# Seven products in place of eight: Strassen's algorithm in one feed-forward stage of a two-layer diffusion backbone

## The chip, the core and the metric

The kernel runs on one core of a Trainium2 chip. The metric is the device time of one execution in microseconds (us). The engines are TensorE (PE in the profile, with PEld for its weight loads), VectorE (DVE), ScalarE (ACT), GpSimd (POOL) and SyncE (SP), which issues the DMAs. Every engine works through its own instructions in their order and waits on semaphores for the others.

## The reference

Two layers work on 512 latent tokens and 256 context tokens, 768 in all, of 1024 channels. Each layer is a feed-forward block (FFN), a mixer and a second FFN. Cut to what matters here:

```python
def half_ffn(x, shift, scale, gate, w1, w3, w2):
    h = modulate(x, shift, scale)
    return x + 0.5 * gate * ((jax.nn.silu(h @ w1) * (h @ w3)) @ w2)
```

`w1` and `w3` (the up projections) are 1024 x 2816, `w2` (the down projection) is 2816 x 1024, all in float32. The first FFN of each layer treats latent and context tokens with the same weights and with different shift, scale and gate.

## The kernel before

Everything is kept with channels on the 128 partitions and tokens along the free dimension. A matrix product in float32 is made of three matmuls on float32r parts: each operand is split into a high part (a rounded copy) and a low part (the operand less that copy), and `mmk` issues high x high, high x low and low x high for each of the k tiles (128 channels each).

**Weights.** The weight tiles (128 x 1024, 512 KB) are used in a planned list, `w_items`. `w_dma` (L190) lets SyncE load one into one of four `raw` buffers. `w_split` (L196) has ScalarE write the high part (L202) and VectorE subtract for the low part (L209, or L207 where it is emitted late). `w_next` (L211) hands out the next tile and first emits the loads and splits that lie ahead of it: with four `hi` and `lo` buffers, up to two tiles ahead.

**The FFN.** The 2816 inner channels are 22 blocks of 128, taken in chunks of 4, 4, 4, 4, 2, 4 blocks. `f1` (L488) does one block: it takes its w1 tile, multiplies it with the context tokens (256 columns) and the latent ones (512 columns), 8 k tiles x 3 matmuls each, lets ScalarE apply silu (L476), does the same with w3, and `gate` (L479) multiplies the two on VectorE (L484), has ScalarE copy the high part (L485) and VectorE subtract for the low part (L486). A block is thus 96 matmuls. `f2` (L513) does the down projection of a whole chunk: for m = 0 to 7 and each group of tokens `down` (L503) sums the chunk's blocks in PSUM, and VectorE adds the result with its gate to the residual (`scalar_tensor_tensor`, L511). `f2` of one chunk is emitted after the first block of the next. The last chunk's is merged with the beginning of the next stage (`post`). PSUM has four buffers for the up projections (`psa`) and four for the down projections (`psb`).

The order of the work is the order in which the program emits it: nothing is reordered. Layer 1's first FFN is the call with `post=self.rw_begin`. Its first two blocks, `first_block`, run while the tokens are being normalised. During layer 0's FFNs and the first part of layer 1 other work, the layers' modulation, is taken from a list `bg` by `ticks`; in layer 1's first FFN that list is empty. The tiles that live through a stage, the activations' parts among them, are 45 slabs of 128 x 768.

Of the kernel before, what the change touches and what calls it, by code (L numbers as in the profile page):

```python
# [7 lines left out]
F32 = mybir.dt.float32  # L8
# [131 lines left out]

class K:
# [10 lines left out]
    # ---------- pools  # L152
# [33 lines left out]
    # ---------- weights  # L186
# [24 lines left out]
    def w_next(self, key, live=0):  # L211
        i = self.w_i
        assert self.w_items[i][0] == key, (self.w_items[i][0], key)
        last = min(i + self.W_SP - 1 - live - 1, len(self.w_items) - 1)
        while self.w_s <= max(last, i):
            while self.w_d <= min(self.w_s + self.W_RAW - 1, len(self.w_items) - 1):
# [4 lines left out]
        while self.w_d <= min(self.w_s + self.W_RAW - 1, len(self.w_items) - 1):  # L221
            self.w_dma(self.w_d)
            self.w_d += 1
        self.w_i += 1
        return self.w_sp.pop(i)
# [28 lines left out]
    # ---------- adaLN  # L254
# [17 lines left out]
    def ada_first(self):  # L272
        """shift and scale of the first FFN, half of the channels at a time: every product on the tensor engine, four column groups at once"""
# [53 lines left out]
    # ---------- norm + modulation: h = x * rsqrt(mean(x^2) + eps) * scale + shift  # L327
# [89 lines left out]
    # ---------- SwiGLU  # L417
    def ffn_items(self, l, i):
        A = self.A
        it = []  # L420
        off = f = 0
# [47 lines left out]
    def ffn(self, l, i, groups, h, post=None, first=None):  # L469
        nc = self.nc  # L470
        gd = 2 if i == 0 else 8
        gs = {}

# [14 lines left out]
        def f1(f, nt):  # L488
# [6 lines left out]
            w = self.w_next(("w3", l, i, f))  # L495
            pss = [self.psa() for g in groups]
# [16 lines left out]
        def f2(c, f0, cf):  # L513
            w = None
            for m in range(8):
                if m % (8 // cf) == 0:
                    w = self.w_next(("w2", l, i, c, m * cf // 8))
# [5 lines left out]
        pend = None  # L523
        for c, cf in enumerate(CHUNKS):
            q = 0
            if c == 0 and first is not None:
# [54 lines left out]
                q = 2  # L581
            while q < cf:
# [10 lines left out]
        c, f0, cf = pend  # L593
        if post is None:
# [31 lines left out]
    # ---------- MLA || conv mixer  # L626
# [40 lines left out]
    def mla(self, h, norm_lat):  # L667
# [54 lines left out]
        # the first two blocks of the convolution's input run while the latent tokens are normalised  # L722
# [34 lines left out]
        # latent projections: kv, q, rope key  # L757
# [58 lines left out]
        # token-major q, k, v  # L816
# [11 lines left out]
        def rot(dst, src, w, t, n, eng):  # L828
            """gain and rotation of n tables' tokens; src and dst [128, n, 32], t the first table, or None where nothing turns"""
# [27 lines left out]
        def prep(p):  # L857
            """closures: transposes, split and row maxima of one pair of heads"""
# [129 lines left out]
        self.plan(self.wout_items() + self.ffn_items(0, 1) + self.ffn_items(1, 0) + self.rwkv_items())  # L988
# [72 lines left out]
        def fin(p):  # L1061
            """closures: one over the sums, and the outputs split"""
# [181 lines left out]
        # output projection  # L1244
# [16 lines left out]
        # the attention's half of the rows first; the first NH blocks of the latent tokens go with the context's  # L1261
# [45 lines left out]
    # ---------- RWKV-7 mixer (second layer)  # L1307
# [22 lines left out]
    def rw_sum(self, kt, g):  # L1330
        """the sum of a token's neighbours"""
# [10 lines left out]
    def rw_diff(self, kt, g):  # L1342
        """half the sum, less the token"""
# [19 lines left out]
    def rw_begin(self, st):  # L1363
        """the context's share of the first products, on the side of the last FFN products"""
# [17 lines left out]
    def rwkv_gemm(self, st):  # L1382
# [101 lines left out]
        def pair(n, j, nxt, at):  # L1484
            """two weight tiles, k outermost; the mixes make room for the next ones"""
# [22 lines left out]
        # keys, and their heads' lengths  # L1508
# [39 lines left out]
        # receptances, and the low-rank branches between them  # L1548
# [77 lines left out]
    def rwkv_prep(self):  # L1626
# [34 lines left out]
        # every operation of this phase as a task of one engine; the order of the tasks is that of a greedy schedule  # L1661
# [5 lines left out]
        def task(key, engs, dur, fn, deps=(), take=(), give=(), u=0, lat=0.2):  # L1667
            """engs: where it may run, dur: how long on each; take, give: the buffers that it claims and frees"""
# [8 lines left out]
        def last(z, key, n):  # L1677
            """a tile that n tasks read"""
# [32 lines left out]
        def dir_tasks(u):  # L1711
# [53 lines left out]
            def k_b():  # L1765
                """b = -2 kk a, from t = tanh(./2), a = (1 + t) / 2"""
# [40 lines left out]
            def gram(b):  # L1807
                """the two heads' products of steps 4b .. 4b + 3 and 12 + 4b .. 12 + 4b + 3"""
# [202 lines left out]
    def run_tasks(self, tasks, free, eng, step, bias, off):  # L2011
        """greedy list schedule: an engine takes the most urgent task whose inputs and buffers are there; then all are emitted in the order of their starts"""
# [47 lines left out]
    def t_batch(self, h, b, eng=None, steps=False):  # L2060
        """(I - L)^-1 of eight steps, both directions and half of the heads: one 32 x 32 block per lane"""
# [31 lines left out]
        def q_mul(x, os=(0, 1)):  # L2093
            """8 x 8 blocks below the diagonal's: W = T L, X = W T"""
# [71 lines left out]
    def t_ticks(self, cost):  # L2166
        """the next of the inverses' operations, as many as hold VectorE for so long"""
# [11 lines left out]
    def rwkv_scan(self):  # L2179
# [11 lines left out]
        def load(g, n):  # L2191
            """two steps of one direction and half of the heads"""
# [545 lines left out]
```

## Time and profile before

| | us |
|---|---|
| median of 3 runs | 3438.64 |
| lowest and highest | 3436.89, 3441.31 |
| profiled execution, first to last instruction (its span; what lies around it isn't given) | 3438.3 |
| TensorE busy | 3168.0 (92%) |
| VectorE busy | 2069.5 (60%) |
| ScalarE busy | 1141.4 (33%) |
| GpSimd busy | 663.6 (19%) |

The profile is that of one execution. In it times run from the first instruction. A row of the timeline gives the start, the duration, the engine, the line of the kernel and the operation with its output and inputs; in brackets stands the idle time before it and what ended it. A matmul's duration reaches from its start to the modelled arrival of its result, so the durations of consecutive matmuls overlap.

### The profile page before, as it was taken

To read this page: it belongs to the slowest core of one execution; us is meant where nothing else is said; L and a number is where in the kernel's file an instruction comes from. 1 tells how busy PE (TensorE), PEld (TensorE's weight loads), DVE (VectorE), ACT (ScalarE), POOL (GpSimd) and SP (SyncE) were. 2 spreads that over 40 slices of the span, in tenths; PEclk is the share of its full clock that TensorE was granted. 3 is DMA by queue.
4 is the path that set the end of the run, shared out by engine and by line. 5 is a ranking of instruction groups with operands and counts; after the bars stand their busy time and mean duration, and the time that the engine had idled before them with its cause. 6 is when DMAs were issued, how large, how long until landed. Compare 5 with 4: busy or idle time off the path is not lost. (4 is left out here: it accounts for less than half of the span.)

```text
span 3438.3 us, 51746 instructions
## 1 busy us (share of the span) xinstructions
PE 3168.0 (92%) x21064; PEld 2636.7 (77%) x21064; DVE 2069.5 (60%) x3246; ACT 1141.4 (33%) x2060; POOL 663.6 (19%) x464
## 2 busy tenths in 40 slices
PE   7999999988989999999999999998786477789999
PEld 6888888874578888888888888776554367678887
DVE  5877734798667776555333343637899775663443
ACT  4122213455543211124122113335564245532222
POOL 1000001356320000002000001215787142230000
PEclk9999999999999999999999999999777689989999
DMA  6444311200133444431111111322587788733222
GB/s 242 146 150 147 132 68 62 78 25 1 47 108 129 141 140 150 146 111 56 68 62 62 62 68 62 109 89 95 149 213 201 186 186 184 165 127 103 98 98 80
DMA packets 251374, 390.59 MB, mean 114 GB/s; under 512 B 67328, under 2 KB 136576, under 8 KB 251136
## 3 DMA queue, kind: packets, MB, share of 16 engines
q1 hardware_dynamic: 251136, 387.28, 36.7%
q8 instruction: 166, 2.72, 0.3%
q14 instruction: 72, 0.59, 0.1%
HBM read 323.24 MB, written 63.96 MB: 113 GB/s over the span
## 5 line engine op out<-in xcount | busy, mean ns | idle before, releaser
L233 PE MATMUL psa<-hhi,whi 128*128 128x512 f32 (+1 forms) x2584 | 893.5, 346 | 6.0 <-ACT whi L202 3.9
L233 PE MATMUL psa<-hlo,whi 128*128 128x512 f32 (+1 forms) x2584 | 894.8, 346 | 2.5 <-POOL hlo L385 2.2
L233 PE MATMUL psa<-hhi,wlo 128*128 128x512 f32 (+1 forms) x2584 | 892.1, 345 | 0.0
L209 DVE TENSOR_TENSOR wlo<-wraw,whi 128x1024 fp32r<-128x1024 f32 (+3 forms) x300 | 366.9, 1225 | 450.5 <-ACT whi L202 450.5
L233 PEld LDWEIGHTS psa<-hhi,whi 128*128 128x128 f32 x2584 | 490.0, 190 | 69.7 <-ACT whi L202 3.9
L233 PEld LDWEIGHTS psa<-hlo,whi 128*128 128x128 f32 x2584 | 489.2, 189 | 67.1 <-POOL hlo L385 4.1
L233 PEld LDWEIGHTS psa<-hhi,wlo 128*128 128x128 f32 x2584 | 489.6, 189 | 61.3
L202 ACT CAST whi<-wraw 128x1024 fp32r<-128x1024 f32 (+2 forms) x345 | 344.6, 1009 | 337.1 <-PE psb L233 198.2
L233 PE MATMUL psb<-ghi,whi 128*128 128x512 f32 (+1 forms) x1232 | 425.6, 345 | 1.4 <-DVE xb L511 0.9
L233 PE MATMUL psb<-glo,whi 128*128 128x512 f32 (+1 forms) x1232 | 424.8, 345 | 0.0
L233 PE MATMUL psb<-ghi,wlo 128*128 128x512 f32 (+1 forms) x1232 | 424.5, 345 | 0.0
L342 POOL TENSOR_TENSOR nacc<-nacc,nsq 128x512 f32<-128x512 f32 (+1 forms) x50 | 56.2, 1125 | 1579.0 <-ACT nsq L338 1574.0
L476 ACT ACTIVATE fs<-psa 128x512 f32<-128x512 f32 (+1 forms) x152 | 77.3, 509 | 576.3 <-PE psa L233 576.2
L485 ACT CAST ghi<-fs 128x512 fp32r<-128x512 f32 (+1 forms) x154 | 81.7, 530 | 552.7 <-DVE fs L484 552.7
L233 PEld LDWEIGHTS psb<-ghi,whi 128*128 128x128 f32 x1232 | 231.9, 188 | 32.8 <-issue 2.2
L233 PEld LDWEIGHTS psb<-ghi,wlo 128*128 128x128 f32 x1232 | 232.0, 188 | 30.0
L233 PEld LDWEIGHTS psb<-glo,whi 128*128 128x128 f32 x1232 | 231.8, 188 | 30.0 <-DVE glo L486 0.3
L484 DVE TENSOR_TENSOR fs<-fs,psa 128x512 f32<-128x512 f32 (+1 forms) x149 | 85.1, 571 | 200.5 <-PE psa L233 197.5
L511 DVE SCALAR_TENSOR_TENSOR xb<-psb,mod,xb 128x256 f32<-128x256 f32 (+1 forms) x192 | 115.7, 614 | 124.5 <-PE psb L233 124.4
L268 DVE CUSTOM_DVE_ANT_0 adaj<-adat,sc,vec 128x512 bf16<-128x512 f32 x224 | 167.9, 750 | 14.7 <-DMA adat<-ada 9.1
L268 DVE CUSTOM_DVE_ANT_0 adaj<-adat,sc,mod 128x512 bf16<-128x512 f32 x224 | 167.9, 750 | 5.9 <-DMA adat<-ada 0.3
L233 PE MATMUL psb<-rhs,lhs 96*32 96x64 f32 (+1 forms) x2560 | 81.1, 241 | 70.4 <-DVE prod L2104 21.4
(398 smaller groups left out, 4907.7 us busy)
## 6 DMA issues: line engine op xcount, KB each, us to landing
wraw<-w SPq DMA_DIRECT2D x264, 512.0 KB
adat<-ada SPq DMA_DIRECT2D x256, 256.0 KB
la_d<-AR SPq DMA_DIRECT2D x32, 384.0 KB
kb_d<-KT SPq DMA_DIRECT2D x16, 768.0 KB
lg_d<-G SPq DMA_DIRECT2D x32, 384.0 KB
lhs<-la_d SPq DMA_DIRECT2D x48, 256.0 KB
lhs<-lg_d SPq DMA_DIRECT2D x48, 256.0 KB
kb<-kb_d SPq DMA_DIRECT2D x48, 256.0 KB
```

Source lines behind the costliest of these rows:

```text
L202: nc.scalar.copy(hi, raw)
L209: nc.vector.tensor_tensor(lo, raw, hi, ALU.subtract)
L233: self.last = self.nc.tensor.matmul(ps, lhsT=lhsT, rhs=rhs, start=start, stop=stop)
L268: nc.vector.tensor_tensor_reduce(out=junk, in0=t, in1=self.sc[cd][hf], scale=1.0, scalar=o if hf else self.col("ada_b", l * 72 + j), op0=A ...
L342: (eng or nc.gpsimd).tensor_tensor(st["acc"], st["acc"], sq, ALU.add)
L476: nc.scalar.activation(s, ps[:, 0:grp[1]], AF.Silu)
L484: nc.vector.tensor_tensor(s, s, ps[:, 0:n], ALU.mult)
L485: nc.scalar.copy(ghi[:, t0:t0 + n], s)
L511: nc.vector.scalar_tensor_tensor(xs, ps[:, 0:n], self.modc(l, gd, m, cd), xs, ALU.mult, ALU.add)
```

## The change

For the last 18 of the 22 blocks, two neighbouring blocks' tiles of one matrix (w1, then w3) are taken as a 2 x 2 matrix: rows are the two blocks, columns the two halves of the 1024 channels. The tokens, all 768 of both kinds, are cut into two halves of 384. The eight half-size products become seven, in the form with four sums on each side (Winograd's variant): A11, A12, S4, S1, S2, S3 and A22 name the weight operand of each. One product is 4 k tiles x 3 matmuls of 384 columns.

- The token side's sums are formed once, by `sums()`: 12 closures in `bg`, taken by the ticks of blocks 2 and 3, and four more (`one`) under the first `f2`. Three of them take 12 more slabs; the fourth is written over a part of `h`.
- The weight side's sums are formed for every pair by VectorE, partly in place in the raw tile. Each operand is 128 x 512 and is split as before; two operands share one `hi` and `lo` tile (a unit). A w2 tile is a unit by itself, loaded through one buffer (`raw2`). `ahead()`, called by every product, emits the split of the next unit if fewer than four are begun; the subtractions for the low parts stay in `late` until the next unit is begun or until `flush_for`. A pair's two raw tiles are loaded two matrices ahead, after S4 of the one before has been split.
- The results are put together on VectorE, from PSUM, in seven additions per matrix, and one copy on ScalarE (`e1`). The last two products of a matrix (`finish`) come in the middle of the next.
- The down projections are as before, but `f2` takes its tiles by `unit()`. It is called within the first w1 of a chunk, between S3 and S1.
- The planned list of weights stops before these blocks (`w_stops`) and goes on with the last chunk's w2 tiles, whose loads `load` emits in place of matrices that are no more there.

A large part of the diff takes comments away. The core of the rest:

```diff
@@ -138,6 +138,312 @@
+class Strassen:
...
+        mats = [(m, f) for f in range(4, NF, 2) for m in ("w1", "w3")]
+        self.mats = mats
...
+        ops = []
+        self.units = []
+        for j, (m, f) in enumerate(mats):
+            ops += [(j, o) for o in ("A11", "S2")]
+            if j:
+                ops += [(j - 1, o) for o in ("A22", "S4")]
+            ops += [(j, o) for o in ("A12", "S3")]
+            if m == "w1" and f in starts:
+                assert len(ops) % 2 == 0
+                ops += [("w2", starts[f] - 1, b) for b in range(CHUNKS[starts[f] - 1])]
+            ops += [(j, "S1")]
+        ops += [(len(mats) - 1, o) for o in ("A22", "S4")]
...
+    def load(self, j):
...
+        self.raw[j] = []
+        for ap in self.src[j]:
+            t = k.wp.tile([128, 1024], F32, tag="raw", bufs=k.W_RAW, name="wraw")
+            self.nc.sync.dma_start(out=t, in_=ap)
+            self.raw[j].append(t)
+    def load2(self):
+        if self.w2_order:
+            o = self.w2_order.pop(0)
+            t = self.raw[o] = self.fp.tile([128, 1024], F32, tag="raw2", bufs=1, name="wraw2")
+            self.nc.sync.dma_start(out=t, in_=self.w2[o[1:]])
+    def split(self):
+        nc, k = self.nc, self.k
+        ops = self.units[self.u]
+        hi = k.wp.tile([128, 1024], F32R, tag="hi", bufs=k.W_SP, name="whi")
+        lo = k.wp.tile([128, 1024], F32R, tag="lo", bufs=k.W_SP, name="wlo")
...
+        if ops[0][0] == "w2":
+            raw = self.raw.pop(ops[0])
+            nc.scalar.copy(hi, raw)
+            def f():
+                TT(lo, raw, hi, ALU.subtract)
+                self.load2()
+            return [f]
+        late = []
+        for q, (j, o) in enumerate(ops):
+            R0, R1 = self.raw[j]
+            a11, a12, a21, a22 = R0[:, 0:512], R0[:, 512:1024], R1[:, 0:512], R1[:, 512:1024]
+            if o == "A11":
+                self.tmp[j] = k.tp.tile([128, 512], F32, tag="t", name="ws1")
+            s1 = self.tmp.get(j)
+            x = {"A11": a11, "S2": a11, "S4": a11, "A12": a12, "A22": a22, "S3": a21, "S1": s1}[o]
+            c = slice(512 * q, 512 * q + 512)
+            h_, l_ = hi[:, c], lo[:, c]
+            if o == "S2":
+                while late:
+                    late.pop(0)()
+                TT(a11, s1, a11, ALU.subtract)
+            nc.scalar.copy(h_, x)
+            if o == "A11":
+                TT(s1, a21, a22, ALU.add)
+                TT(a21, a11, a21, ALU.subtract)
+            def f(o=o, j=j, x=x, h_=h_, l_=l_, a11=a11, a12=a12):
+                TT(l_, x, h_, ALU.subtract)
+                if o == "S2":
+                    TT(a11, a12, a11, ALU.subtract)
+                if o == "S4":
+                    self.raw.pop(j)
+                    self.load(j + 2)
+                if o == "S1":
+                    del self.tmp[j]
+            late.append(f)
+        return late
+    def ahead(self):
+        if self.u < len(self.units) and len(self.sp) < self.k.W_SP:
+            self.flush()
+            self.late = self.split()
+    def begin(self):
+        self.load(0)
+        self.load(1)
+        self.load2()
+        for _ in range(2):
+            self.ahead()
+        self.flush()
+    def unit(self, o):
+        u, q = self.at[o]
+        while self.u <= u:
+            self.flush()
+            self.late = self.split()
+        self.flush_for(u)
+        hi, lo = self.sp[u]
+        self.left[u] -= 1
+        if not self.left[u]:
+            del self.sp[u]
...
+    def flush_for(self, u):
+        if u == self.u - 1:
+            self.flush()
...
+        def s1(kt):
+            tiles[kt] = [plain(kt, tA), plain(kt, tB), plain(kt + 4, tA), plain(kt + 4, tB)]
+        def s2(kt):
+            r11, r12, r21, r22 = tiles[kt]
+            TT(r11, r12, r11, ALU.subtract)
+            TT(r12, r22, r12, ALU.subtract)
+            TT(r22, r22, r11, ALU.subtract)
+            TT(r21, r21, r22, ALU.subtract)
+        def s3(kt):
+            r11, r12, r21, r22 = tiles.pop(kt)
+            for o, x in ((2, r22), (3, r12), (4, r21)):
+                t = k.slab([128, NT], F32R, f"ht{o}")
+                self.T[o, kt] = t[:, 0:n], t[:, n:2 * n]
+                split(x, *self.T[o, kt])
+        k.bg += [lambda f=f, kt=kt: f(kt) for kt in range(4) for f in (s1, s2, s3)]
+        def one(kt):
+            a, b = plain(kt, tA), plain(kt, tB)
+            TT(b, b, a, ALU.subtract)
+            split(b, hhi[kt][:, tB], hlo[kt][:, tB])
+        self.one = [lambda kt=kt: one(kt) for kt in range(4)]
...
+    def product(self, j, o):
+        k = self.k
+        w = self.unit((j, o))
+        self.ahead()
+        ps = k.psa()
+        for kt in range(4):
+            k.mmk(ps[:, 0:self.n], w, kt, self.rhs(o, kt), kt == 0, kt == 3)
+        return ps
...
+    def out(self, j, blk, x):
+        nc, k = self.nc, self.k
+        m, f = self.mats[j]
+        if m == "w1":
+            nc.scalar.activation(x, x, AF.Silu)
+            self.s[blk] = x
+            return
+        s = self.s.pop(blk)
+        f += blk[0]
+        if f not in self.gs:
+            self.gs[f] = (k.slab([128, NT], F32R, "ghi"), k.slab([128, NT], F32R, "glo"))
+        hi, lo = (t[:, self.tt[blk[1]]] for t in self.gs[f])
+        nc.vector.tensor_tensor(s, s, x, ALU.mult)
+        nc.scalar.copy(hi, s)
+        nc.vector.tensor_tensor(lo, s, hi, ALU.subtract)
...
+    def finish(self, j, u2, u3):
+        self.add(u3, self.product(j, "A22"), u3)
+        self.out(j, (1, 0), u3)
+        self.add(u2, self.product(j, "S4"), u2)
+        self.out(j, (0, 1), u2)
+    def matrix(self, m, f, between):
+        k = self.k
+        j = self.mats.index((m, f))
+        e1 = self.e()
+        self.nc.scalar.copy(e1, self.product(j, "A11")[:, 0:self.n])
+        u2 = self.e()
+        self.add(u2, self.product(j, "S2"), e1)
+        if self.old:
+            old, self.old = self.old, None
+            self.finish(*old)
+            del old
+        self.add(e1, self.product(j, "A12"), e1)
+        self.out(j, (0, 0), e1)
+        e1 = None
+        u3 = self.e()
+        self.add(u3, self.product(j, "S3"), u2)
+        if between:
+            if self.one:
+                k.bg += self.one
+                self.one = None
+            between()
+        ps = self.product(j, "S1")
+        c22 = self.e()
+        self.add(c22, ps, u3)
+        self.add(u2, ps, u2)
+        self.out(j, (1, 1), c22)
+        self.old = j, u2, u3
+    def end(self):
+        self.finish(*self.old)
+        self.old = None
+        self.flush()
+        self.T.clear()
+        self.k.w_pre()()
+        self.k.w_pre()()
+        self.close()
...
@@ -493,6 +809,8 @@
             w = self.w_next(("w3", l, i, f))
+            if fast and f == 3:
+                fx.begin()
@@ -514,15 +832,30 @@
                 if m % (8 // cf) == 0:
-                    w = self.w_next(("w2", l, i, c, m * cf // 8))
+                    w = None
+                    w = fx.unit(("w2", c, m * cf // 8)) if fast else self.w_next(("w2", l, i, c, m * cf // 8))
                 for g in groups:
                     down(f0, cf, m, w, g)
                 self.ticks(1)
 
...
+            if fast and c > 0:
+                for q in range(0, cf, 2):
+                    for n in ("w1", "w3"):
+                        fx.matrix(n, f0 + q, f2_pend if pend else None)
+                pend = (c, f0, cf)
+                f0 += cf
...
+                if fast:
+                    fx.sums()
...
         c, f0, cf = pend
+        if fast:
+            fx.end()
...
@@ -985,7 +1325,11 @@
-        self.plan(self.wout_items() + self.ffn_items(0, 1) + self.ffn_items(1, 0) + self.rwkv_items())
+        self.plan(self.wout_items() + self.ffn_items(0, 1))
+        it, tail = self.ffn_items(1, 0, True)
+        self.plan(it)
+        self.w_stops.append(len(self.w_items))
+        self.plan(tail + self.rwkv_items())
...
-    nc = bacc.Bacc("TRN2", target_bir_lowering=False, num_devices=1)
+    nc = bacc.Bacc("TRN2", target_bir_lowering=False, num_devices=1, dynamic_dma_scratch_size=1024)
```

## Rows read from the trace of the kernel before

**Rows 1.** The page's first line: span and instructions.
```profile
span 3438.3 us, 51746 instructions
```
**Rows 2.** Windows: stretch, length, busy time (instructions) by engine, clock, DMA share, GB/s.
```profile
1600.00:2120.00 520.00, 519.16 (x2965) 453.59 (x2964) 179.79 (x247) 110.90 (x158) 5.20 (x4) 1.00 0.18 61
```
**Rows 3.** Waits of TensorE, 1600 to 2120: total us, times, longest.
```profile
PE psa L233 <- POOL hlo L385: 0.8, 1, 0.8
```
**Rows 4.** Timeline of TensorE: the first of 12, 12 and 12 matmuls.
```profile
1700.48 0.28 PE L233 MATMUL psb<-ghi,whi 128*128 128x256 f32 x1
...
1701.89 0.40 PE L233 MATMUL psb<-ghi,whi 128*128 128x512 f32 x1
...
1704.66 0.28 PE L233 MATMUL psb<-ghi,whi 128*128 128x256 f32 x1
```
**Rows 5.** Timeline of ScalarE: the first silu of a block, three blocks apart.
```profile
1716.06 0.39 ACT L476 ACTIVATE fs<-psa 128x256 f32<-128x256 f32 x1 [10.39 <-PE psa L233]
...
1766.52 0.39 ACT L476 ACTIVATE fs<-psa 128x256 f32<-128x256 f32 x1 [0.59 <-PE psa L233]
```
**Rows 6.** Groups by shape, 1700 to 2000: count, busy us, mean ns, idle before.
```profile
L202 ACT CAST whi<-wraw 128x1024 fp32r<-128x1024 f32 x36 | 37.4, 1047 | 58.6 <-PE psb L233 43.8 <-issue 14.8
...
L486 DVE TENSOR_TENSOR glo<-fs,ghi 128x512 fp32r<-128x512 f32 x12 | 8.3, 692 | 8.3 <-ACT ghi L485 8.3
L484 DVE TENSOR_TENSOR fs<-fs,psa 128x512 f32<-128x512 f32 x12 | 8.3, 688 | 50.9 <-PE psa L233 50.9
L485 ACT CAST ghi<-fs 128x512 fp32r<-128x512 f32 x12 | 7.5, 623 | 65.1 <-DVE fs L484 65.1
...
L484 DVE TENSOR_TENSOR fs<-fs,psa 128x256 f32<-128x256 f32 x12 | 5.1, 421 | 0.3
L485 ACT CAST ghi<-fs 128x256 fp32r<-128x256 f32 x12 | 4.9, 408 | 20.7 <-DVE fs L484 20.7
```
**Rows 7.** Timeline of VectorE within a down projection.
```profile
1704.86 0.75 DVE L511 SCALAR_TENSOR_TENSOR xb<-psb,mod,xb 128x512 f32<-128x512 f32 x1 [2.29 <-PE psb L233]
1705.53 1.22 DVE L209 TENSOR_TENSOR wlo<-wraw,whi 128x1024 fp32r<-128x1024 f32 x1
1706.66 0.48 DVE L511 SCALAR_TENSOR_TENSOR xb<-psb,mod,xb 128x256 f32<-128x256 f32 x1
```
**Rows 8.** Timeline of VectorE: an operation and the one that reads its result.
```profile
578.82 0.30 DVE L384 CAST hhi<-nxr 128x256 fp32r<-128x256 f32 x1 [0.34 <-ACT nxr L377]
579.15 0.42 DVE L385 TENSOR_TENSOR hlo<-nxr,hhi 128x256 fp32r<-128x256 f32 x1
```
**Rows 9.** Timeline of VectorE: one gate of 512 columns.
```profile
1730.03 0.69 DVE L484 TENSOR_TENSOR fs<-fs,psa 128x512 f32<-128x512 f32 x1 [4.24 <-PE psa L233]
1731.41 0.69 DVE L486 TENSOR_TENSOR glo<-fs,ghi 128x512 fp32r<-128x512 f32 x1 [0.69 <-ACT ghi L485]
```
**Rows 10.** Windows of 1 us around a load: the last two numbers are DMA.
```profile
1707.00:1708.00 1.00, 1.00 (x6) 0.83 (x5) 0.14 (x1) 0.00 (x0) 0.00 (x0) 1.00 0.34 70
1708.00:1709.00 1.00, 1.00 (x7) 0.82 (x6) 0.00 (x0) 0.00 (x0) 0.00 (x0) 1.00 0.89 336
1709.00:1710.00 1.00, 1.00 (x11) 1.00 (x10) 0.75 (x1) 0.00 (x0) 0.00 (x0) 1.00 0.30 119
```
**Rows 11.** Windows around two waits of TensorE; the clock is third from last.
```profile
576.00:578.00 2.00, 1.07 (x7) 0.99 (x8) 0.43 (x2) 0.68 (x2) 0.00 (x0) 1.00 0.03 8
578.00:580.00 2.00, 2.00 (x7) 1.56 (x6) 1.63 (x6) 1.16 (x3) 0.00 (x0) 0.56 0.00 0
580.00:582.00 2.00, 2.00 (x7) 1.57 (x6) 1.83 (x6) 1.14 (x2) 0.73 (x1) 0.58 0.00 0
...
2131.00:2134.00 3.00, 1.93 (x15) 1.76 (x15) 1.04 (x3) 0.78 (x2) 0.00 (x0) 1.00 0.23 87
2134.00:2137.00 3.00, 3.00 (x15) 2.43 (x14) 2.42 (x7) 2.58 (x10) 1.55 (x3) 1.00 0.00 0
```

More of the change, by code (lines that the diff above doesn't have):

```diff
@@ L214, in w_next @@
         last = min(i + self.W_SP - 1 - live - 1, len(self.w_items) - 1)
+        stops = self.w_stops
+        while stops and i >= stops[0]:
+            stops.pop(0)
+        end = min(len(self.w_items), stops[0] if stops else 1 << 30)
+        last = min(last, end - 1)
         while self.w_s <= max(last, i):
-            while self.w_d <= min(self.w_s + self.W_RAW - 1, len(self.w_items) - 1):
+            while self.w_d <= min(self.w_s + self.W_RAW - 1, end - 1):
                 self.w_dma(self.w_d)
@@ L220, in w_next @@
             self.w_s += 1
-        while self.w_d <= min(self.w_s + self.W_RAW - 1, len(self.w_items) - 1):
+        while self.w_d <= min(self.w_s + self.W_RAW - 1, end - 1):
             self.w_dma(self.w_d)
@@ L415, in norm_all, with ffn_items @@
             self.norm_h(st, kt, l, c0, h)
-    def ffn_items(self, l, i):
+    def ffn_items(self, l, i, fast=False):
         A = self.A
         it = []
+        if fast:
+            it = [((n, l, i, f), A[n][l, i, f].rearrange("p k m -> p (k m)"), 1024) for f in range(4) for n in ("w1", "w3")]
+            off = 128 * 1024 * sum(CHUNKS[:-1])
+            return it, [(("w2", l, i, len(CHUNKS) - 1, b), A["w2"][l, i, off + b * 131072:off + (b + 1) * 131072].rearrange("(p n) -> p n", p=128), 1024) for b in range(4)]
         off = f = 0
@@ L467, in first_block, with ffn @@
                 fin(j)
-    def ffn(self, l, i, groups, h, post=None, first=None):
+    def ffn(self, l, i, groups, h, post=None, first=None, fast=False):
         nc = self.nc
@@ L472, in ffn @@
         gs = {}
+        fx = self.strassen(l, i, groups, h, gs) if fast else None
         def silu(ps, grp):
@@ L523, in ffn, with f2_pend @@
         pend = None
+        def f2_pend():
+            nonlocal pend
+            f2(*pend)
+            for f in range(pend[1], pend[1] + pend[2]):
+                del gs[f]
+            pend = None
         for c, cf in enumerate(CHUNKS):
             q = 0
+            if fast and c > 0:
[4 more added lines that the diff above has]
+                f0 += cf
+                continue
             if c == 0 and first is not None:
@@ L593, in ffn @@
         c, f0, cf = pend
+        if fast:
+            fx.end()
         if post is None:
@@ L624, in ffn, with strassen @@
         return sts[-1]
+    def strassen(self, l, i, groups, h, gs):
+        return Strassen(self, l, i, groups, h, gs)
     def mla_items(self):
@@ L2560, in body @@
         self.w_i = self.w_s = self.w_d = 0
+        self.w_stops = []
         self.cp, c_cp = self.open("cp", 1, side="left")
@@ L2692, in body @@
         st0 = st
-        st = self.ffn(1, 0, [CTX, LAT], h, post=self.rw_begin, first=self.hook(st0, 1, 0, h))
+        st = self.ffn(1, 0, [CTX, LAT], h, post=self.rw_begin, first=self.hook(st0, 1, 0, h), fast=True)
         self.dump_x("x4")
```

85 lines of the change are left out of this document (added).

## The prediction

> **What bounds the kernel now.** I read the page first: one core, span 3438.3 us [rows 1], which is 0.3 us under the median of the runs shown (3438.64), so sums are made against the span and 0.3 is added. The change lies in one stage, layer 1's first FFN. The view by windows finds it at about 1600 to 2120 us: TensorE is busy 519.2 of 520 us at granted clock 1.00, VectorE 180, ScalarE 111 [rows 2]. The waits of TensorE in that stretch come to one of 0.8 us [rows 3]. So the stage lasts as long as its matmuls take to issue, and the other engines are hidden. A matmul saved there is time saved, and a new wait of TensorE there is time added in full.
>
> **What goes.** Durations of matmuls overlap, so I take start-to-start times. Twelve of 256 columns take 1701.89 - 1700.48 = 1.41 us (0.1175 each), the next twelve, of 512, take 1704.66 - 1701.89 = 2.77 us (0.2308) [rows 4]. That is 0.44 ns a column and almost nothing fixed. No 384-column matmul is in the trace; these two rows are its ends, and it lies halfway in columns, so I take 0.1742. One block (w1 and w3, 96 matmuls) takes (1766.52 - 1716.06)/3 = 16.82 us from first silu to first silu [rows 5]; 18 blocks are 302.8 us. After, 9 pairs of blocks x 2 matrices x 7 products = 126 products of 12 matmuls, each product 12 x 0.1742 = 2.09 us, together 263.4: 39.4 less. If what a block holds above its 96 x 0.1742 grows with the products, it is an eighth of 302.8, 37.9. I take **38 off** (37 to 41).
>
> **What comes, where TensorE must wait.** A 512-wide subtraction on VectorE lasts 0.69, a 256-wide 0.42 [rows 6]; 384 is halfway, 0.56. One that waits for nothing new starts 0.08 before its forerunner's end: 1704.86 + 0.75, next at 1705.53 [rows 7]. One that needs the forerunner's result starts 0.03 after its end: 578.82 + 0.30, next at 579.15 [rows 8]. A PSUM result is taken 0.20 us after the next matmul started (1704.66 and 1704.86) [rows 4, 7].
>
> (a) *The fourth w2 tile.* Products call ahead(), the loop f2 doesn't. With four split buffers all four w2 units are begun before f2, but the subtraction of the fourth is still held in `late`, and is emitted by unit() ahead of its first matmul, behind m = 5's scalar_tensor_tensor, which waits for TensorE. TensorE has two matmuls on the high half, then waits: 0.20 + 0.67 + 1.22 [rows 7] + 0.05 - 0.23 = 1.9 us. Before, this subtraction ran under m = 4 [rows 7]. Four f2's have four w2 tiles (chunks 0 to 3): 7.6.
>
> (b) *The product after f2.* By then nothing is split ahead. S1's unit also holds the next matrix's A11, whose two sums come first: last scalar_tensor_tensor, two sums, S1's subtraction: 0.20 + 0.67 + 0.61 + 0.61 + 0.69 + 0.05 - 2 x 0.174 = 2.5 us, four times: 9.9. After chunk 4 (two w2 tiles) units are left over: 0.
>
> (c) *The end.* end() splits the last w2 tiles only behind the last gate: add and product 0.59 each, ScalarE's copy 0.43 until the next can start, its copy of w2 1.09, subtraction 1.22, with 0.20 and 0.05 at the ends, less two matmuls 0.23: 3.9.
>
> (d) *The start.* The 12 closures of sums() fill the four up projections of blocks 2 and 3 (33.4 us): each k has 11 VectorE operations of 384 columns, and three wait for ScalarE's copy; 4 x 6 us. With 4 whole weight subtractions (4.6), the first two units' 4 half ones and 4 sums (4.9) and two blocks' gates (some 6) VectorE has some 39 us there, 6 too many; it is late gates and psum that TensorE then meets. I take 2 (0 to 5).
>
> (e) *VectorE's queue.* Per matrix: 7 subtractions and 4 sums at 0.61, 7 PSUM additions at 0.475, 2 gates. A gate runs product, ScalarE copy, subtraction, with VectorE idle between, as at 1730.03 to 1731.41 for 512 columns [rows 9]; with 384: 0.56 + 0.51 + 0.07 + 0.47 = 1.6. Together 6.7 + 3.3 + 3.2 = 13.2 us, against 7 x 2.09 = 14.65 on TensorE, where it was a third busy [rows 2]. And the queue is in order, with a DMA in it: load(j+2) goes out after S4's subtraction of matrix j. A 512 KB tile lands 2.6 us after its buffer is free (subtraction ends 1706.75 [rows 7], last bytes in 1709 to 1710 at 336 GB/s before [rows 10]); two tiles, 4.2 us. After f2, where units are split one per product, A11's sums meet that load and VectorE falls some 4 us behind; later each load costs it about 0.7. Per four matrices, with three w2 subtractions: 4 x 13.9 + 3.4 = 59.0 against 58.6. So it stays 4 to 5 us behind until the next f2, where it has slack. Four psum buffers bear about 6. Laid out one after another, the 28 products run into it once, where e1's copy stands on ScalarE behind a copy that waits for a load: 2 us a chunk, **8.6 in all** (0 to 25). ScalarE has 7 x 0.53 + 5 x 0.42 = 5.8 us a matrix, hidden. SyncE's issues move with the subtractions; nothing else is in its queue there. The adaLN loads are over by then, and the smaller DMA scratch carries no transfer of this kernel, whose DMAs all go out on SyncE's queue: 0.
>
> (f) *The clock.* A wait of 1.07 us ahead of four small matmuls was followed by granted clock 0.56 and 0.58 in the next four microseconds: 3.4 us at the lower level (1.2 GHz), 1.7 us lost [rows 11]. Another such wait, with 1.93 of 3 us busy, was not [rows 11]. The waits above are longer, some 13 of 1.9 us and more; I let 5 of them cost 1.7: 8.5 (0 to 22).
>
> Sum: 7.6 + 9.9 + 3.9 + 2 + 8.6 + 8.5 = 40.5 on, 38 off: 3438.3 + 0.3 + 2.5 = **3441 us**.
>
> **A rule weighed.** VectorE's spacing decides (e), and the rows show an independent instruction starting 0.08 us before its forerunner's end [rows 7]. The Trainium skill, VectorE: DVE Perf Modes, section "The DRAIN you can't avoid", says that the next operation does not start until the pipeline is empty. Rows 7 differ from that for two operations without a common operand, and the sum goes by the rows. [...]
>
> **The rivals.** *First, faster:* the queue never binds and the clock stays up. For it: a lag of 4 to 5 us is under what four buffers bear, and not every wait lowered the clock [rows 11]. Against it: 59.0 against 58.6 leaves nothing. Then only (a), (b), (c) remain: 38 - 21.4 = 16.6 off, **3422**. *Second, slower:* VectorE sets the pace of the up projections. Place: the stretch between two f2's. At whole durations a matrix is 11 x 0.69 + 7 x 0.56 + 2 x 1.7 = 14.9, with 0.7 for the load 15.6, against 14.65: 3.8 us more than TensorE per four matrices, and 3.7 for w2. On top of the 4.3 behind from the first load, less the 6 that buffers bear, TensorE waits 5.8 a chunk, not 2. Over 4.5 chunks 16 more: **3457**. It decides from about 13.9 us a matrix upward; each 0.1 us beyond costs 1.8 us in all. For it: many of the new operations need the one before or ScalarE's answer [rows 8, 9]. Against it: f2 gives back some 20 us of VectorE's time. *Third:* the smaller count isn't shorter, if a 384-column matmul took 0.200 and not 0.174: 126 x 12 x 0.026 = 39 more, 3480. Only a kink between the rows' two sizes could do that.
>
> **How the numbers follow.** Forecast 0.38, first rival 0.29, second 0.29, third 0.04. The forecast's own range is 3431 to 3451. The 80% range has to reach the first two rivals: from 3420 (a, b, c alone and the larger gain) to 3464 (second rival with five more low stretches of the clock). A run of this kernel tells about 0.2%, 7 us, from no change. Of the forecast's 0.38 I put 0.03 below 3431.7 and 0.02 above 3445.5; with the rivals: faster 0.32, same 0.33, slower 0.35.
>
> **What would show it.** Matmuls of 384 columns spaced 0.174; the stretch's matmul count down by an eighth of the up projections; among TensorE's waits four of about 1.9 on w2's low half, four of 2.5 on S1's, one near 4 at the end; VectorE 80 to 90% busy between f2's, with psum waits of TensorE on ScalarE's e1 or VectorE's additions; PEclk under 1.00 in some windows. No waits after f2 would refute (b) and give the first rival; many waits of TensorE on VectorE throughout the up projections would give the second.

## The result, and the profile after

The changed kernel takes 3459.36 us (median of 5 runs, 3454.27 to 3469.68) against 3438.64 (median of 5 runs beside it, 3436.89 to 3444.83): ratio 1.0067, 95% interval 1.0049 to 1.0084. It is slower by 20.7 us where 2.5 were forecast. The range, 3420 to 3464, holds the time; the likeliest case's own range, 3431 to 3451, does not.

The whole stage is read with one window in each kernel, from the matmul that waits for GpSimd's `hlo` [rows 3] to the first matmul of the next stage's norm. The columns are those of [rows 2]. Before:

```profile
1609.80:2133.10 523.30, 521.73 (x2984) 456.17 (x2984) 180.48 (x249) 111.70 (x163) 8.32 (x9) 1.00 0.18 63
```

After:

```profile
1612.30:2157.70 545.40, 502.98 (x2768) 464.86 (x2768) 352.71 (x597) 159.94 (x287) 8.31 (x9) 0.97 0.18 61
```

The page's first line, which answers to [rows 1]:

```profile
span 3457.5 us, 51829 instructions
```

The 216 matmuls that were to go are gone (2984 to 2768; an eighth of 18 x 96). The stage is 22.1 us longer all the same: TensorE is not busy for 42 us of it where it was for 1.6, and the mean granted clock fell from 1.00 to 0.97. Outside the stage the two profiles differ by 2.5 us before it and 5.4 the other way behind it (span 3457.5 less 2157.7, against 3438.3 less 2133.1). The profiles of other kernels, whose work ahead of the stage is the same, begin it anywhere from 1605.6 to 1614.5, so the first is no effect of the change. Behind the stage lie 1305.2 us in both profiles without the products (before, and x4_scratch below) and 1296.1 to 1304.1 in the eleven with them, so the second may in part be one; it was not followed.

The waits of TensorE from 1640 to 2156 (total us, times, longest) where [rows 3] had one of 0.8:

```profile
PE psa L544 <- DVE wlo L268: 12.6, 5, 3.0
PE psb L544 <- ACT ghi L396: 8.2, 4, 3.6
PE psb L544 <- DVE wlo L244: 7.0, 4, 1.7
PE psb L544 <- DVE xb L829: 3.8, 1, 3.8
PE psa L544 <- ACT e L413: 3.2, 3, 1.6
PE psb L544 <- ACT whi L508: 2.8, 1, 2.8
PE psa L544 <- DVE e L400: 1.1, 2, 0.6
PE psb L544 <- DVE wlo L513: 0.8, 1, 0.8
...
```

L268 is the subtraction of a weight operand of the products, L244 that of a w2 tile, L396 ScalarE's copy in a gate, L829 the addition to the residual, L413 the copy e1, L400 the additions from PSUM, L508 and L513 the split of the last w2 tiles. The view counts idle time from a matmul's modelled end, so I also add up *lost issue time*: what lies between the starts of consecutive matmuls beyond the normal 0.1175, 0.1742 or 0.2308 us for 256, 384 or 512 columns. Over the stage it is 5.1 us before and 64.9 after, 59.8 more. It holds waits and matmuls at the lower clock alike. The stage grew by 22.1, so the products' saving was 59.8 - 22.1 = 37.7 us. Everything that follows is about the 60.

### The profile page after: what moved, and what is told of

Its sections match the earlier page's. It is cut to its first block, busy times and chain, and to the rows that moved or that the text cites. A ratio compares the mean times of both kernels' runs of the same rounds, so it can differ in the third digit from the quotient of the medians.

```text
span 3457.5 us, 51829 instructions
## 1 busy us (share of the span) xinstructions
PE 3153.6 (91%) x20848; PEld 2650.6 (77%) x20848; DVE 2242.9 (65%) x3594; ACT 1186.7 (34%) x2184; POOL 664.9 (19%) x464
## 5 line engine op out<-in xcount | busy, mean ns | idle before, releaser
L544 PE MATMUL psa<-hhi,whi 128*128 128x512 f32 (+2 forms) x2296 | 799.7, 348 | 11.2 <-ACT whi L508 3.9
L544 PE MATMUL psa<-hhi,wlo 128*128 128x512 f32 (+2 forms) x2296 | 798.4, 348 | 9.7 <-DVE wlo L268 9.7
L544 PE MATMUL psa<-hlo,whi 128*128 128x512 f32 (+2 forms) x2296 | 800.2, 349 | 2.5 <-POOL hlo L696 2.3
L515 DVE TENSOR_TENSOR wlo<-wraw,whi 128x1024 fp32r<-128x1024 f32 (+2 forms) x244 | 298.7, 1227 | 306.5 <-ACT whi L508 306.4
L544 PEld LDWEIGHTS psa<-hhi,whi 128*128 128x128 f32 x2296 | 437.7, 191 | 65.4 <-ACT e L413 4.2
L544 PEld LDWEIGHTS psa<-hhi,wlo 128*128 128x128 f32 x2296 | 437.9, 191 | 59.8 <-DVE wlo L268 11.0
L544 PEld LDWEIGHTS psa<-hlo,whi 128*128 128x128 f32 x2296 | 437.2, 190 | 55.2 <-POOL hlo L696 4.2
L508 ACT CAST whi<-wraw 128x1024 fp32r<-128x1024 f32 (+3 forms) x291 | 287.9, 1000 | 254.8 <-PE psb L544 132.7
L801 ACT CAST ghi<-fs 128x256 fp32r<-128x256 f32 (+1 forms) x118 | 62.9, 533 | 414.3 <-DVE fs L800 414.3
L792 ACT ACTIVATE fs<-psa 128x256 f32<-128x256 f32 (+1 forms) x116 | 59.4, 512 | 421.5 <-PE psa L544 421.5
L829 DVE SCALAR_TENSOR_TENSOR xb<-psb,mod,xb 128x256 f32<-128x256 f32 (+1 forms) x192 | 115.6, 615 | 133.5 <-PE psb L544 133.5
```

The source lines that it names most:

```text
L508: nc.scalar.copy(hi, raw)
L515: nc.vector.tensor_tensor(lo, raw, hi, ALU.subtract)
L544: self.last = self.nc.tensor.matmul(ps, lhsT=lhsT, rhs=rhs, start=start, stop=stop)
L792: nc.scalar.activation(s, ps[:, 0:grp[1]], AF.Silu)
L801: nc.scalar.copy(ghi[:, t0:t0 + n], s)
L829: nc.vector.scalar_tensor_tensor(xs, ps[:, 0:n], self.modc(l, gd, m, cd), xs, ALU.mult, ALU.add)
```

## The experiments

**Was it the empty split buffers behind a down projection?** Theory: most of the lost time stems from f2 not calling `ahead()`. Rival: VectorE sets the pace, and splitting earlier only moves the waits.

```diff
                     down(f0, cf, m, w, g)
+                if fast and c < len(CHUNKS) - 1:
+                    fx.ahead()
                 self.ticks(1)
```

> f2 calls ahead() after every m, so that splitting goes on during the down projections; nothing else differs from the changed kernel. Theory (waits of TensorE for splits that are emitted just in time): the four waits of 1.90 us on the fourth w2 tile and the four of 2.58 us on S1's low half go, 17.9 us of issue time, and with them some of the half-rate stretches of the clock: about 3437 to 3441. Rival (VectorE's queue sets the pace of the up projections): the splits are only moved, the waits come back as waits for psum buffers between two f2's, and the time stays above 3450.

Measured: 3421.07 us (5 runs, ratio 0.9952, interval 0.994 to 0.9964), faster than before, by more than the theory gave. The stage, and TensorE's waits from 1640 to 2117:

```profile
1605.60:2118.70 513.10, 498.15 (x2767) 465.62 (x2767) 351.86 (x597) 163.65 (x287) 8.33 (x9) 0.97 0.18 64
```

```profile
PE psb L544 <- DVE xb L829: 5.7, 3, 3.1
PE psa L544 <- DVE wlo L268: 3.0, 1, 3.0
PE psb L544 <- ACT whi L508: 2.7, 1, 2.7
...
PE psb L544 <- ACT ghi L396: 0.2, 1, 0.2
```

The waits of 1.9 and 2.6 us are gone, as expected; so are all waits for PSUM results and all but 0.2 of the 8.2 us of waits for a gate (1.7 of 10.6 in lost issue time), which the theory had left standing. VectorE does the same work (351.9 us against 352.7). The lost time falls from 64.9 to 32.8. (The stage is 10.2 us shorter than before's, the median 16.5; in the other kernels stage and median differ from before's by amounts that agree to 3 us, here they are 6 apart, which comes from outside the stage and was not followed.) ScalarE still waits for the w2 loads with a gate's copy behind it, but nobody is waiting for that copy any more:

```profile
1767.49 1.05 ACT L241 CAST whi<-wraw 128x1024 fp32r<-128x1024 f32 x1 [4.44 <-DMA wraw<-w]
1768.44 0.51 ACT L396 CAST ghi<-e 128x384 fp32r<-128x384 f32 x1
```

So a good part of what I had put down to a full VectorE was the start without anything split: VectorE and ScalarE run late from there until the next f2. The rival, waits moved to the PSUM buffers and over 3450, falls.

**Is it enough to begin f2 with the held subtraction?** The same wait, taken away in another way.

```diff
             w = None
+            if fast:
+                fx.flush()
             for m in range(8):
```

> f2 begins by emitting the subtractions still held in `late`, and does not split ahead; nothing else differs from the changed kernel. It takes away the waits for the fourth w2 tile (7.6 us) alone. Theory (the emptied lookahead after f2 is what makes VectorE late in the up projections): the four waits of 2.58 on S1's low half, the waits for psum and those for the gates' high parts stay, so 7 to 10 us less than the changed kernel, about 3450. Rival (any VectorE work taken out of its late place frees the queue): the gates' and psum waits go as well, under 3440.

Measured: 3462.94 us (6 runs, 1.0069, 1.0054 to 1.0084). That is a miss: about 3450 was expected, and the time is the changed kernel's within the noise. The waits for w2's low half are gone, others have come for them:

```profile
PE psb L544 <- DVE xb L829: 12.9, 5, 7.7
PE psa L544 <- DVE wlo L268: 12.7, 5, 3.0
PE psb L544 <- ACT ghi L396: 7.1, 4, 2.7
...
```

The subtraction now stands at the head of f2 in VectorE's queue and waits there for the load, and the additions that free the PSUM buffers stand behind it:

```profile
1798.15 1.23 DVE L244 TENSOR_TENSOR wlo<-wraw,whi 128x1024 fp32r<-128x1024 f32 x1 [4.09 <-ACT whi L241]
...
1799.83 0.39 PE L544 MATMUL psb<-ghi,whi 128*128 128x256 f32 x1 [2.17 <-DVE xb L829]
```

In the changed kernel, holding it back in `late` cost no more than this. The part that the theory left standing (L268, gates) did stay.

**Is VectorE's load needed for the lag?** This kernel leaves out the sums on the weight side, 72 operations of VectorE, and so computes something else.

```diff
-                TT(a11, s1, a11, ALU.subtract)
+                pass
...
-                TT(s1, a21, a22, ALU.add)
-                TT(a21, a11, a21, ALU.subtract)
+                pass
...
-                    TT(a11, a12, a11, ALU.subtract)
+                    pass
```

> Leaves out the four sums of every matrix on the weight side (72 VectorE operations, 44 us of its time), so the seven products are of the raw quarters and the output is not the reference's; every copy, subtraction, load, product and addition stays. Theory (single waits, VectorE's queue mostly bears its lag): the waits on S1's low half shrink by the two sums ahead of it, 1.2 us each, those for psum in the up projections go (5 us), those for w2 and the gates stay: 8 to 14 us less, about 3447. Rival (VectorE sets the pace): most of what is lost comes back, 25 us or more, below 3435.

Measured: 3427.46 us (6 runs, 0.9971, 0.9958 to 0.9984), between x1 and the changed kernel. By the time alone this is the rival's case (below 3435), not the theory's 3447. Waits from 1640 to 2120:

```profile
PE psa L543 <- DVE wlo L267: 7.3, 5, 3.0
PE psb L543 <- DVE wlo L244: 7.0, 4, 1.7
PE psb L543 <- DVE xb L828: 3.1, 2, 2.5
...
```

The four waits for a w2 tile are untouched, those ahead of S1 are shorter by the two sums, 1.25 in place of 2.6 us of lost issue each. The waits for gates and PSUM results are gone here too. So the lag needs both, the start without lead and the 44 us of sums; taking away either one ends it. (Part of this kernel's gain is the clock, which falls at one place in the stage here and at six in the changed kernel.) My expectation had these as alternatives, which they are not.

**The load of w2.** Two kernels. In one the high part's copy of a w2 tile is held in `late` with the subtraction, so that on ScalarE no gate stands behind a copy that waits for a load. In the other w2 has a second buffer, made of two half-width tiles, so that every other w2 tile is loaded, copied and subtracted in two halves.

```diff
             raw = self.raw.pop(ops[0])
-            nc.scalar.copy(hi, raw)
             def f():
+                nc.scalar.copy(hi, raw)
                 TT(lo, raw, hi, ALU.subtract)
```

> ScalarE's copy of a w2 tile's high part is emitted when its subtraction is, two products later, in place of ahead of them; nothing else differs from the changed kernel. Theory (the gates' copies stand on ScalarE behind a copy that waits for a DMA): the first down projections' waits for the gate's high part, 10.6 us of issue time in all, go down to under 3, and the time to about 3445 to 3450. Rival (those waits come from VectorE being late): they stay within 3 us of what they were, and the time at 3457 to 3460.

Measured: 3449.77 us (8 runs, 1.0038, 1.0023 to 1.0052), a time as the theory had it. Three of the four waits for a gate are gone; the last one grew from 3.7 to 4.7 us of lost issue, so that 5.4 of the 10.6 are left where the theory had under 3:

```profile
PE psb L544 <- ACT ghi L396: 4.5, 1, 4.5
```

```diff
+            self.n2 = getattr(self, "n2", 0) + 1
+            if self.n2 % 2:
...
+            else:
+                self.raw[o] = [(slice(512 * q, 512 * q + 512), self.k.tp.tile([128, 512], F32, tag="acc", bufs=2, name="wraw2")) for q in range(2)]
...
         self.load2()
+        self.load2()
```

> The changed kernel with a second buffer for w2 tiles (two 128 x 512 tiles that lie idle in this stage), so that a load is issued two w2 tiles ahead and not one; nothing else differs. Theory (f2 leaves nothing split, and that, not the loads, makes VectorE late): the gates' waits at the first down projection, 10.6 us, and the 3.95 of the start go for the most part, because ScalarE's copies no longer stand behind a load; the waits of 1.90 and 2.58 stay (17.9 us): about 3445. Rival (the chain of w2 loads is the whole cause of the lag): the psum waits go as well, and the time comes near the kernel before, 3438 or less.

Measured: 3442.58 us (11 runs, 1.0007, 0.9997 to 1.0017), near the theory's 3445. Waits from 1640 to 2132:

```profile
PE psa L554 <- DVE wlo L277: 12.6, 5, 3.0
PE psb L554 <- DVE wlo L252: 4.8, 4, 1.2
PE psa L554 <- ACT e L423: 3.3, 3, 1.2
...
PE psb L554 <- ACT ghi L406: 0.8, 1, 0.8
...
```

The waits for gates go from 8.2 to 0.8, so they were the load; the waits ahead of S1 and those for e1 stay within a tenth of a microsecond, so they were not. The waits for w2's low half, which the theory let stand, fall from 1.90 to 1.37 us of lost issue each, and that is not the second buffer: the fourth tile's subtraction is in two halves of 0.68 us here, and TensorE goes on after the first (1700.63 to 1701.37 in the first f2).

**The smaller DMA scratch alone**, in the kernel before:

```diff
-    nc = bacc.Bacc("TRN2", target_bir_lowering=False, num_devices=1)
+    nc = bacc.Bacc("TRN2", target_bir_lowering=False, num_devices=1, dynamic_dma_scratch_size=1024)
```

> The kernel before with only the smaller DMA scratch. Theory: no effect, within 0.1% of the kernel before, about 3439. Rival (the changed kernel was already 2.5 us late when the stage began, which the scratch caused): 3441 or more.

Measured: 3438.43 us (11 runs, 1.0004, 0.9995 to 1.0012). No cost of it is to be seen.

**The two ends of the stage.** On top of `ahead()` in f2, the last units' subtractions and the last w2 tiles' splits are emitted before the last two products.

```diff
             self.late = self.split()
+        elif self.u == len(self.units):
+            self.flush()
...
     def end(self):
-        self.finish(*self.old)
-        self.old = None
         self.flush()
-        self.T.clear()
         self.k.w_pre()()
         self.k.w_pre()()
+        self.finish(*self.old)
+        self.old = None
+        self.T.clear()
```

> x1_ahead, and at the end: ahead() emits what is held in `late` when there is no unit left to begin, and the splits of the last two w2 tiles are emitted ahead of the last two products in place of behind them. Theory (these splits are late only by their place): the waits of 3.13, 2.91 and 0.76 go, 6.8 us, with 5 us of half clock: about 3410. Rival (the last chunk's gates hold the first down projection anyway): a wait of 2 us or more comes in their place, and 3417 or more.

Measured: 3416.03 us (6 runs, 0.9942, 0.9927 to 0.9958), between the theory's 3410 and the rival's 3417; from x1 the runs hardly tell it apart, the trace does. The end's 6.8 us of lost issue became 2.3 (1.79 on a gate, 0.48); the start's 7.5 became 9.6, which I had not expected. Two more kernels went after the start: no `ahead()` in the first matrix once three units are begun, and then two of the four plain additions of `sums()` on GpSimd as well.

```diff
         w = self.unit((j, o))
-        self.ahead()
+        if j or self.u < 3:
+            self.ahead()
```

> x6_ahead_end, and the first matrix's products begin no w2 unit but the first; the others are begun in the first f2. Theory (VectorE's queue stands behind three loads of w2 one after another, 4 us each, ahead of the residual's additions): the waits of 2.19 and 3.23 at the first f2 go, and 3 to 5 us of half clock: 7 to 9 us less than x6. Rival (the four token sums in that f2, or the late gates of block 3, are what holds it): under 3 us less.

```diff
-            tiles[kt] = [plain(kt, tA), plain(kt, tB), plain(kt + 4, tA), plain(kt + 4, tB)]
+            r22 = plain(kt + 4, tB, nc.gpsimd)
+            r21 = plain(kt + 4, tA, nc.gpsimd)
+            tiles[kt] = [plain(kt, tA), plain(kt, tB), r21, r22]
```

> x7_ahead_end_start, and two of the four additions that begin each k's token sums run on GpSimd, which is idle there. Theory (the twelve closures overfill VectorE by some 6 us in blocks 2 and 3): the waits of 0.81, 0.42 and 0.82 for the sums and the gate go, 2 us and a stretch of half clock: 2 to 4 us less than x7. Rival (GpSimd takes longer for one than VectorE saves, or both slow each other down): no gain, or 2 us more.

Measured: 3423.64 us (5 runs, 0.9955, 0.9943 to 0.9967) and 3422.05 (6 runs, 0.9952, 0.9938 to 0.9966). Both miss: the start's waits of 4.13, 2.48 and 0.90 turn into five of 0.55 to 1.98, and two more come later. Neither another order of VectorE's work at the start nor less of it took the waits away.

**All together, with the second w2 buffer:** x6 and x9 in one kernel, and then with GpSimd's additions.

> x6_ahead_end with the second buffer for w2 tiles. Theory: the waits of 4.13, 2.48 and 0.90 at the first f2, where three w2 loads follow one another with VectorE behind them, shrink to under 2, with 3 us of half clock: 6 to 9 us less than x6, about 3408. Rival (the token sums in that f2 and the late gates hold it): under 2 us less.

> x10_ahead_end_two, and two of the four additions that begin each k's token sums on GpSimd. Theory: 1 to 3 us less than x10 (the waits of 0.80, 0.43 and 0.82 at the end of block 3 shrink). Rival: no gain, as in x8.

Measured: 3406.05 us (5 runs, 0.9911, 0.9897 to 0.9925) and 3405.0 (4 runs, 0.9906, 0.9893 to 0.992), both faster than before and the changed kernel. The first is as the theory had it; what the second adds, 1 us, is inside the noise. The stage of the first of them, and TensorE's one wait within it, from 1640 to 2105, that is over 0.7 us (a gate):

```profile
1613.60:2106.80 493.20, 488.07 (x2767) 458.82 (x2767) 352.99 (x606) 165.54 (x296) 8.31 (x9) 0.99 0.20 67
```

```profile
PE psb L556 <- ACT ghi L408: 1.6, 1, 1.6
```

The stage is 30.1 us shorter than before's, with 353 us of VectorE in 493. The start's waits add up to 2.0 us of lost issue here, against 9.6 with one w2 buffer: what x7 and x8 had missed was the load.

## Why the prediction came out as it did

The terms of the sum beside the lost issue time that the trace of after shows:

| | predicted us | measured us |
|---|---|---|
| the products' saving | 38 | 37.7 |
| (a) fourth w2 tile | 7.6 | 1.90 + 1.89 + 1.90 + 1.90 = 7.6 |
| (b) S1 after f2 | 9.9 | 2.57 + 2.59 + 2.59 + 2.59 = 10.3 |
| (c) the end | 3.9 | 2.99 + 0.92 = 3.9 |
| not in the sum: A22 of the last matrix | 0 | 3.1 |
| (d) the start | 2 (0 to 5) | 0.80 + 0.42 + 0.82 + 3.95 = 6.0 |
| (e) VectorE's queue | 8.6 (0 to 25) | 10.6 at gates, 5.2 for PSUM results = 15.8 |
| (f) the clock | 8.5 (0 to 22) | 13.6 |
| sum | 40.5 | 60.3 |

Of the 64.9 us, what is left is 4.6, about the 5.1 that the kernel before has as well.

That the range holds 3459 is in part luck: its upper end was set for the second rival, whose mechanism did not come, with five more low stretches of the clock.

**The saving was right.** A 384-column matmul lies between its neighbours [rows 4]: from the first to the thirteenth of a run, 12 of them take 2.11 us, 0.176 each (mean of the stage 0.1748), and the third rival falls.

```profile
1831.95 0.34 PE L544 MATMUL psa<-hhi,whi 128*128 128x384 f32 x1
...
1834.06 0.34 PE L544 MATMUL psa<-hhi,whi 128*128 128x384 f32 x1
```

**(a), (b) and (c) were right, mechanism and size.** S1's chain is as it was laid out, the last addition to the residual, two sums, the subtraction, and TensorE after it:

```profile
1821.07 0.75 DVE L829 SCALAR_TENSOR_TENSOR xb<-psb,mod,xb 128x512 f32<-128x512 f32 x1 [2.27 <-PE psb L544]
1821.73 0.68 DVE L264 TENSOR_TENSOR ws<-wraw 128x512 f32<-128x512 f32 x1
1822.45 0.69 DVE L265 TENSOR_TENSOR wraw<-wraw 128x512 f32<-128x512 f32 x1
1823.06 0.68 DVE L268 TENSOR_TENSOR wlo<-ws,whi 128x512 fp32r<-128x512 f32 x1
...
1823.80 0.44 PE L544 MATMUL psa<-hhi,wlo 128*128 128x384 f32 x1 [2.43 <-DVE wlo L268]
```

The cause of (a) and (b) is shown by x1, which takes them away by splitting during f2; that of (c) by x6, which splits the last w2 tiles earlier and leaves 2.3 us at the end.

**One wait was overlooked.** `ahead()` is also what emits the held subtractions, and does nothing when no unit is left. A22 and S4 of the last matrix are then split when they are needed, behind the last S1's additions: 3.1 us. With x6's two lines it is gone. Part (c) looked at the w2 tiles of `end()` alone.

**(e) had the right kind of wait, half its size, and one place too few.** The step that failed is the load, its length and what was looked for behind it. I took 2.6 us for a tile, from the end of the subtraction that frees the buffer to the last bytes [rows 7, 10]. From the issue to the start of the copy that uses it, it takes 3.3 us (1776.40 to 1779.72; the 13 w2 loads of the stage that ScalarE waits for take 3.2 to 3.4, one of them 4.9), and two tiles 4.8 to 5.6 (the longest: issue 1828.84, VectorE's sum at 1834.46), not 4.2. The two tiles, and then SyncE's issue of a w2 tile, ScalarE, VectorE and then TensorE at the second down projection:

```profile
1828.84 0.93 SPq L220 DMA_DIRECT2D wraw<-w  x2
...
1834.46 0.69 DVE L264 TENSOR_TENSOR ws<-wraw 128x512 f32<-128x512 f32 x1 [2.58 <-DMA wraw<-w]
...
1776.40 0.33 SPq L227 DMA_DIRECT2D wraw<-w  x1
...
1779.72 1.05 ACT L241 CAST whi<-wraw 128x1024 fp32r<-128x1024 f32 x1 [4.75 <-DMA wraw<-w]
1780.68 0.51 ACT L396 CAST ghi<-e 128x384 fp32r<-128x384 f32 x1
1786.28 1.05 ACT L241 CAST whi<-wraw 128x1024 fp32r<-128x1024 f32 x1 [5.09 <-DMA wraw<-w]
1787.23 0.51 ACT L396 CAST ghi<-e 128x384 fp32r<-128x384 f32 x1
...
1783.41 0.56 DVE L395 TENSOR_TENSOR e<-e 128x384 f32<-128x384 f32 x1
1787.77 0.56 DVE L397 TENSOR_TENSOR glo<-e,ghi 128x384 fp32r<-128x384 f32 x1 [3.80 <-ACT ghi L396]
...
1787.79 0.50 PE L544 MATMUL psb<-ghi,whi 128*128 128x512 f32 x1 [1.08 <-ACT ghi L396]
```

The product of the gate is done at 1783.97, its copy starts at 1787.23, because ScalarE's queue holds the copy of the next w2 tile, and that waits for its load; so does the gate's subtraction on VectorE, and what is behind that. I had looked for this only where e1's copy stands behind a load (2 us a chunk; measured 5.2 over the stage for all PSUM results) and not at the gates that f2 reads first (10.6, gone but for one in x2 and in x9). They need the lag as well: x1 ends them with the loads as they are. VectorE's own durations were right: 551 to 558 ns for 384 columns, where 0.56 was taken; between f2's it is busy 84% (40.12 of 48 us from 1726 to 1774).

**(d) failed at the same step.** I counted VectorE's work at the start, 39 us in 33.4, and the 2 us put on that are there (0.80 + 0.42 + 0.82). The other 3.95 come from what I did not count, the subtractions in its queue that each wait for a w2 load; with the second buffer, in x9 and x10, this wait is gone. It stands idle there while it is late (start, duration, and in brackets the idle time):

```profile
1680.34 1.23 DVE L244 TENSOR_TENSOR wlo<-wraw,whi 128x1024 fp32r<-128x1024 f32 x1 [3.92 <-ACT whi L241]
1686.06 1.22 DVE L244 TENSOR_TENSOR wlo<-wraw,whi 128x1024 fp32r<-128x1024 f32 x1 [4.03 <-ACT whi L241]
```

**(f) had nearly the number of places, five for six, and not their length.** Windows of 2 us, with one less the granted clock as the lost share, give 13.6 us in six places of after and nothing in before. Two of the six lost about 3.4 us each where I took 1.7 for all. One of these, after a wait of 3.56 us for a gate (the clock is third from last):

```profile
2058.00:2062.00 4.00, 0.99 (x8) 0.78 (x6) 3.89 (x6) 0.90 (x3) 0.00 (x0) 1.00 0.00 0
2062.00:2066.00 4.00, 3.44 (x9) 2.66 (x10) 3.43 (x7) 1.45 (x3) 0.00 (x0) 0.50 0.02 4
2066.00:2070.00 4.00, 4.00 (x18) 3.47 (x17) 2.15 (x4) 0.71 (x2) 0.00 (x0) 0.64 0.00 0
```

Of the eight waits of 1.74 and 2.41 to 2.43 us in (a) and (b) two went with the lower level (1.2 GHz), of the five of 2.58 and more four. That fits [rows 11], where one wait of two was. Most of this term goes when the waits go: the same sum over x10 gives 3.4.

**The rivals.** The second rival's time, 3457, is close to the measured one, and its mechanism isn't what happened. (By its own figures, (5.8 - 2) x 4.5, the 16 us are 17, and the time 3458.) It had every operation of VectorE cost its whole duration. After repeats [rows 7]: two independent subtractions take 1.29 us for 0.69 each, so the second starts 0.60 after the first, and two additions of 384 columns 1.02.

```profile
1771.37 1.29 DVE L268 TENSOR_TENSOR wlo<-wraw,whi 128x512 fp32r<-128x512 f32 x2
1772.57 1.02 DVE L400 TENSOR_TENSOR e<-psa,e 128x384 f32<-128x384 f32 x2
```

The section of the Trainium skill that the prediction weighed, VectorE: DVE Perf Modes, "The DRAIN you can't avoid", goes on, behind the sentence on the empty pipeline, to say that a next operation that is not held starts earlier. The prediction left that out; with it the Trainium skill gives no ground for whole durations, and these rows, of operations that wait for nothing, agree with it. The kernel x1 settles it in another way: the same VectorE work, and TensorE waits for none of it between f2's. The first rival had the queue never bind. It did, in the changed kernel; with the lead kept through f2 it doesn't, and x1's 3421 is near that rival's 3422 only by coincidence, since x1 has no (a) and (b) and keeps the waits at both ends and 13.7 us of lower clock.

So the sum was short by some 20 us (40.5 for 60.3): 11 from the w2 load and the queues behind it (7.2 in (e), 4.0 in (d)), 3.1 from the overlooked place, 5.1 from the clock. How much of the 11 is the load's greater length, and how much the places that were not looked at, is not shown: no run has a shorter load. Why the first three w2 loads hit harder in x6 than in x1 (9.6 against 7.5 us at the start) was not separated; that a second buffer ends it was.

## What to carry to other kernels

A step that splits or loads ahead has to be called in every phase that uses up what lies ahead, the short one between two loops too; where it isn't, the consumer pays the chain once there, and all engines behind it are late afterwards. Follow a load from its issue to the start of its first user, and list what stands behind that user in its queue, on each engine: here a gate that had nothing to do with w2 paid for w2. And when TensorE saves 38 us by matmuls that need 172 us more of VectorE, price the slack of each queue per phase, not over the stage: over the stage there was plenty.

## What was not expected of the hardware

A 512 KB load on SyncE's queue has its user start 3.3 us after the issue, two of them 4.8 to 5.6; the bytes alone, by windows, had looked like 2.6, and 4.2 was worked out for two. The lower clock cost more after single waits than [rows 11] had shown: 13.6 us in a stage with 46.7 us of waits, and between two kernels that lose 65 and 33 us in the stage it was the same, 13.6 and 13.7, so it did not go by their sum. Nor did it go by the length of a wait alone: the three waits of 0.80, 0.42 and 0.82 us at the start are in the changed kernel, x1, x2, x9 and x10 alike, and the granted clock fell behind them in x1, x2 and x10 only.
